# Sixteen rounds of value pages joined to eight pairs, in a decoder step on one core

## The chip, the core and the metric

The kernel runs on one core of one Trainium2 chip. The metric is the device time of one execution in microseconds (us); lower is better. Engines are named as the profile names them: PE is TensorE with its matrix products, PEld its loading of the stationary operand, DVE is VectorE, ACT is ScalarE, POOL is GpSimd, SP is SyncE, which here only issues transfers.

## What is computed

One layer of a decoder for 256 prompt tokens and 8 sequences of 4 new tokens (288 columns in all), model width 2048, in float32. The reference, cut to what matters:

```python
hp = ffn_half(hp, norm_ffn1[l], w_ffn1_gate[l], w_ffn1_up[l], w_ffn1_down[l])
cb, u, q, k, v, logf = mixer_in(hp, norm_mix[l], w_in[l], b_f[l])      # one projection, w_in
conv_y = cb * short_conv(u_ext, conv_w[l])
attn_o = fox_prompt(q, k, v, logf)
hp = mixer_out(hp, conv_y, attn_o, norm_conv_out[l], norm_attn_out[l], w_out[l])
hp = ffn_half(hp, norm_ffn2[l], ...)
hp = ple_add(hp, p_prompt[l], norm_ple[l], w_ple_gate[l], w_ple_proj[l])
# the new tokens go the same way, with this attention:
v_past = cache_v[page_table].reshape(DB, P, N_HEADS, HEAD_DIM)
s = jnp.einsum('bqhd,bkhd->bhqk', q, k_all, ...) * SCALE
s = s + Fq[..., None] - F[:, :, None, :]
p = jax.nn.softmax(s, axis=-1)
return jnp.einsum('bhqk,bkhd->bqhd', p, v_all)
```

The change touches the last line for the new tokens: probabilities times the values of the past. The past is 1024 rows a sequence, in 8 pages of 128 rows x 8 heads x 128 features, 0.524 MB each; 8 sequences have 64 pages, and a page table says where each lies.

## The kernel before

The 288 columns go through the whole layer together. A projection is made in output pairs of 2 x 128 rows, and a pair in **chunks**: four blocks of 128 input rows by 256 output columns, 0.524 MB of weights that SP loads into a place `raw0` to `raw7` (L238 to L247). ACT and DVE split every weight into a high and a low part (`whi`, `wlo`, L288), and PE makes three products for each block (L333 to L335), 24 for a chunk. The split runs up to five half chunks ahead of PE.

The order of the work in the mixing stage is written out by hand. A list `fill` holds the chunks: those of the keys, of the convolution's inputs, of the values and the first half of the output projection. A table `marks` says what stands ahead of chunk i: `at(i, f)` puts f at place i (L1003), and `between` (L978) merges both. `run_steps` (L352) goes through the steps, and ahead of each it asks for the loads of the next `state["ahead"]` items (`load_upto`, L232). An item is a weight, four key pages or, in this version, one value page. Each engine takes its instructions in the order that the scheduler of the framework makes of this; waits are put in by it.

The value pages go into eight places: `raw4` to `raw7`, three of their own (`v0` to `v2`) and `wideb` (`page_tile`, L260). From then on weights have only `raw0` to `raw3`, until the last round is done. The request for a page is an indirect transfer issued by POOL (L255), one instruction each, in POOL's order with its other work: the multiplications of the convolution (L901 to L945), the masks of the prompt's attention (L844, L845), the sums of squares (L889) and the additions into h (L1013).

The 64 pages are used in 16 **rounds** (`v_round`, L785): two groups of four sequences, eight rounds each, four pages a round, one of each sequence. A round is eight products of 32 columns by 512 on the four column groups of PE (`tile_position`), which the trace shows as 16 instructions at L794. They add up in two PSUM banks `va` through the eight rounds of a group; `sample_out` (L802) then adds the products with the new rows, and DVE picks out the heads. The rounds stand at places 51, 53, 56, 59, 61, 64, 67, 69, 72, 75, 78, 80, 83, 86, 88 and 91 (`VSTEP`, L1046), among `probs_t` (places 50 and 52), which transposes the probabilities, the natural forms of the values (L666), eight `prompt_head` (places 69, 71, 74, 76, 79, 81, 84, 86) and two norms. `v_start` (L966) at place 48 opens the stage and sets the lookahead to 12 items.

Of the kernel before, what the change touches and what calls it, by code (L numbers as in the profile page):

```python
# [36 lines left out]
PAGES = 8  # L37
# [10 lines left out]
KSTEP = 3  # L48
WEIGHTS = 4
VPAGES = 3  # L50
AHEAD = 12
WARM = (NT, NT, NT, P // 2)
VSTEP = 2.7

GAINS = ("norm_mix", "norm_ffn2", "norm_ple", "norm_final", "norm_conv_out", "norm_attn_out", "conv_w")
A_ROWS = dict(norm_mix=D, norm_ffn2=D, norm_ple=D, norm_final=D, norm_conv_out=CB * P, norm_attn_out=NH * P,
# [37 lines left out]
def build(nc, tc, ctx, A, O):  # L94
# [3 lines left out]
    v, s, g, pe, sy = nc.vector, nc.scalar, nc.gpsimd, nc.tensor, nc.sync  # L98
# [8 lines left out]
    def bank(tag, bufs):  # L107
        return ps.tile([P, 512], F32, name=tag, tag=tag, bufs=bufs)
# [28 lines left out]
    at = 0  # L137
# [15 lines left out]
    idx = cst.tile([P, 64], I32, name="idx")  # L153
# [76 lines left out]
    state = dict(wslot=0, pages=0, through=False, ahead=RAW, loaded=0, split=0, used=0, halves_used=0, chunk=0, lead=HALVES)  # L230

    def load_upto(n, parts=None):  # L232
        while state["loaded"] < min(n, len(items)):
            it = items[state["loaded"]]
            if it["kind"] == "p" and "vx" not in W:
                return
            if it["kind"] == "w":
                state["wslot"] = (state["wslot"] + 1) % (WEIGHTS if state["pages"] and not state["through"] else RAW)  # L238
                t = rawp.tile([P, it["nk"], 256], F32, name="wraw", tag=f"raw{state['wslot']}")
                src = it["src"]  # L240
                if parts is not None:
                    cuts = (0, 1, 2, 3, 4) if state["loaded"] < 2 else (0, 2, 4)
                    parts.append([(t[:, a:b], src[:, a:b]) for a, b in zip(cuts, cuts[1:])])
                else:
                    d = sy.dma_start(t, src)
                    if state["used"] < 24:
                        tc.keep_in_program_order(d)  # L247
            elif it["kind"] == "k":
                t = W["kt"][0].tile([P, 4, NH, P], F32, name="KT", tag="KT", bufs=2)
                for i, r in enumerate(it["rows"]):  # L250
                    g.indirect_dma_start(out=t[:, i].rearrange("p h s -> p (h s)"), out_offset=None, in_=it["src"],  # L251
                                         in_offset=bass.IndirectOffsetOnAxis(ap=r, axis=0))
            else:
                t = page_tile()
                g.indirect_dma_start(out=t, out_offset=None, in_=it["src"],  # L255
                                     in_offset=bass.IndirectOffsetOnAxis(ap=it["rows"], axis=0))
            it["tile"] = t
            state["loaded"] += 1

    def page_tile():  # L260

        own = ([(rawp, f"raw{i}") for i in range(WEIGHTS, RAW)] + [(W["vx"][0], f"v{i}") for i in range(VPAGES)]
               + [(W["mix"][0], "wideb")])
        n = state["pages"]
        state["pages"] += 1
        p, tag = own[n] if n < len(own) - 1 else own[(n + 1) % len(own)]
        return p.tile([P, 9 * P] if tag == "wideb" else [P, NH * P], F32, name="page", tag=tag)[:, :NH * P]

    halves = []
# [1 line left out]
    def split_upto(n):  # L271
        while state["split"] < min(n, len(halves)):
            it, j = halves[state["split"]]
            if "tile" not in it:
                return
            x = it["tile"][:, j:j + 2, :]
            hi = wsp.tile([P, 2, 256], F32R, name="whi", tag="whi")
            lo = wsp.tile([P, 2, 256], F32R, name="wlo", tag="wlo")
            if state["split"] < 4:
                it["parts"][j] = (hi, lo)  # L280
                state["split"] += 1
                continue
            split_weight(hi, lo, x, state["split"] < 14)
            it["parts"][j] = (hi, lo)
            state["split"] += 1
# [11 lines left out]
    def weight(src, k0, nk, c0):  # L297
        if len(src.shape) == 5:
            part = src[c0 // 256, k0 // 4]
        else:  # L300
            part = src[k0 * P:(k0 + nk) * P, c0:c0 + 256].rearrange("(k p) c -> p k c", p=P)
        return dict(kind="w", src=part, nk=nk, parts={})

    def page(src, j):
        return dict(kind="p", src=src, rows=idx[:, j:j + 1])

    def pair(src, c0, kts, act, evac, k_of=lambda k: k, late=0, tag="mm", rows_first=False):

        st = {}
        out = []  # L310
        chunks = [kts[i:i + 4] for i in range(0, len(kts), 4)]
        for ci, ks in enumerate(chunks):
            it = weight(src, ks[0], len(ks), c0)

            def fn(ci=ci, ks=ks, it=it, only=None):
                if ci == 0 and not only:
                    st["ps"] = [bank(tag, BANKS[tag]) for _ in range(2)]
                last = ci == len(chunks) - 1
                if only is None:
                    split_upto(state["halves_used"] + state["lead"])  # L320
                if not only:
                    state["chunk"] += 1
                for b in range(2):
                    o = st["ps"][b][:, :NT]
                    for j, k in enumerate(ks):
                        if only not in (None, j):
                            continue
                        hi, lo = it["parts"][j // 2 * 2]
                        w = slice(b * P, b * P + P)
                        xh, xl = act(k_of(k))  # L330
                        f = ci == 0 and j == 0
                        l = last and j == len(ks) - 1
                        pe.matmul(o, hi[:, j % 2, w], xh, start=f, stop=False)  # L333
                        pe.matmul(o, hi[:, j % 2, w], xl, start=False, stop=False)  # L334
                        pe.matmul(o, lo[:, j % 2, w], xh, start=False, stop=l)  # L335
                    if only not in (None, len(ks) - 1):
                        continue
                    if b == 0:
                        run_deferred()
                    if last and late:  # L340
                        defer(lambda b=b, o=o: evac(b, o), late)
                    elif last:
                        evac(b, o)
                state["halves_used"] += len(ks) // 2 if only is None else only % 2

            if rows_first:
                out.extend(([] if j else [it], lambda j=j, fn=fn: fn(only=j)) for j in range(len(ks)))
                continue
            out.append(([it], fn))
        return out  # L350

# [18 lines left out]
    def defer(fn, chunks=1):  # L370

        deferred.append((state["chunk"] + chunks, fn))

    def run_deferred(force=False):
        due = [d for d in deferred if force or d[0] <= state["chunk"]]
        for d in due:
            deferred.remove(d)
        for _, fn in due:
            fn()
# [55 lines left out]
    W = {}  # L435

    def opened(name, side="left"):
        st = ExitStack()
        W[name] = (pool(name, to=st, side=side), st)
# [91 lines left out]
    M = {}  # L531
# [250 lines left out]
                              t[:NS, :P].rearrange("s (c b x) -> s b c x", c=4, b=4)[:, b])  # L782
        M["PT", gi] = pt

    def v_round(gi, r):  # L785
        its = [page(A["cache_v"], (4 * gi + b) * PAGES + r) for b in range(4)]

        def fn():
            if r == 0:
                M["va", gi] = [bank("va", BANKS["va"]) for _ in range(2)]  # L790
                M["pv", gi] = M["PT", gi].rearrange("s (r b x) -> s r b x", b=4, x=32)
            for e in range(2):
                for b in range(4):
                    pe.matmul(M["va", gi][e][32 * b:32 * b + 32, :], M["pv", gi][:, r, b],  # L794
                              its[b]["tile"][:, e * 512:e * 512 + 512], start=r == 0, stop=False, tile_position=(0, 32 * b))
            if r == PAGES - 1:
                if gi == 1:
                    state.update(through=True, wslot=WEIGHTS - 1)
                sample_out(gi)
        return (its, fn)  # L800

    def sample_out(gi):  # L802
        mx = W["vv"][0]
# [162 lines left out]
    def v_start():  # L966
# [4 lines left out]
        opened("vx", "right")  # L971
        state["ahead"] = AHEAD
        vv = W["vv"][0]
# [29 lines left out]
    def at(i, *fns):  # L1003
        marks.setdefault(i, []).extend(fns)
# [37 lines left out]
    at(48, v_start)  # L1042
    at(50, lambda: probs_t(0))
    at(52, lambda: probs_t(1))
    for r in range(2 * PAGES):
        at(int(51 + VSTEP * r), v_round(r // PAGES, r % PAGES))  # L1046
    for hh in range(NH):
        at(int(69 + 2.5 * hh), lambda hh=hh: prompt_head(hh))
    at(80, lambda: norm_scale(rsc, acc2, CB * P, 2))
# [159 lines left out]
```

## Time and profile before

| | us |
|---|---|
| median of 3 runs | 2327.54 |
| lowest and highest | 2327.27, 2327.67 |
| the profiled execution | 2327.59 |
| its span, first to last instruction | 2325.8 |

The profile is one execution with the hardware profiler. Its rows read: start and length in us (timeline), engine, line of the kernel, operation, result and operands by the program's names, shape and count. A row of waits reads: who, waited for whom, us in total, times, longest. A row of a stretch reads: from and to, length, the busy time and number of instructions of PE, PEld, DVE, ACT and POOL, the granted clock of PE, the busy share of the 16 DMA engines, and GB/s. Queue q0 has POOL's transfers (among them the pages), q1 SP's (the weights). The stage with the value pages takes from about 1071 us, when the first page is asked for, to 1283 us.

### The profile page before, as it was taken

The numbers are of one execution on the slowest core, as the hardware profiler recorded it, in microseconds if no ns is written. First come the engines' busy times: TensorE is split into PE (matmuls) and PEld (weight loads), VectorE is DVE, ScalarE is ACT, GpSimd is POOL, SyncE is SP. The second block draws the span as 40 slices with busy tenths as digits, with TensorE's granted clock in tenths as the row PEclk, the third lists the DMA queues.
The fourth block names the chain that finished last, engine by engine and source line by source line (L and its number), as shares of the span: only waits on it lengthen the run. The fifth ranks groups of instructions, "written<-read, shape, count | busy, mean of one in ns | idle before, by whom it ended". The sixth has DMA issues, their size and how long they took to land.

```text
span 2325.8 us, 44305 instructions
## 1 busy us (share of the span) xinstructions
PE 2312.2 (99%) x17389; PEld 2254.0 (97%) x17389; DVE 1342.3 (58%) x2413; ACT 1057.1 (45%) x1864; POOL 323.9 (14%) x398
## 2 busy tenths in 40 slices
PE   9999999999999999999999999999999999999997
PEld 9999999999999999888888999999999999999997
DVE  7555555555555586456466765555555555555755
ACT  7444444444444453334344554444434444444654
POOL 1020000000000013444445210000000000000110
PEclk9999999999999999999999999999999999999999
DMA  8575555555555547997988555545555555555552
GB/s 273 164 238 166 166 167 164 164 165 166 167 164 164 163 163 232 330 318 262 321 316 295 164 165 158 176 155 172 163 166 164 170 164 164 164 165 167 164 166 91
DMA packets 342865, 443.44 MB, mean 191 GB/s; under 512 B 17424, under 2 KB 306976, under 8 KB 342656
## 3 DMA queue, kind: packets, MB, share of 16 engines
q1 hardware_dynamic: 320944, 366.32, 49.6%
q0 software_dynamic: 20480, 71.67, 9.0%
q8 instruction: 136, 2.23, 0.4%
q10 hardware_dynamic: 1232, 2.62, 0.3%
q14 instruction: 73, 0.60, 0.1%
HBM read 435.48 MB, written 5.07 MB: 189 GB/s over the span
## 4 chain that ended last, share of the span: by engine, by line
PE 99%; DVE 0%; ACT 0%; issue 0%; DVEq 0%
PE mm L333 31%; PE mm L335 31%; PE mm L334 31%; PE va L794 1%; PE va L736 1%; PE va L333 1%; PE va L335 1%; PE va L334 1%; DVE h L1135 0%; PE kt L335 0%; PE kt L333 0%; PE kt L334 0%; PE mm L509 0%; PE kt L848 0%; PE kt L881 0%; PE kt L872 0%
## 5 line engine op out<-in xcount | busy, mean ns | idle before, releaser
L288 DVE TENSOR_TENSOR wlo<-wraw,whi 128x512 fp32r<-128x512 f32 (+1 forms) x1388 | 973.0, 704 | 800.4 <-ACT whi L288 745.5
L288 ACT ACTIVATE whi<-wraw 128x512 fp32r<-128x512 f32 (+1 forms) x1388 | 866.3, 629 | 932.8 <-PE mm L334 864.0
L333 PE MATMUL mm<-xh,whi 128*128 128x288 f32 x3680 | 1094.3, 297 | 0.2 <-DVE uc L922 0.2
L334 PE MATMUL mm<-xl,whi 128*128 128x288 f32 x3680 | 1085.7, 295 | 0.0
L335 PE MATMUL mm<-xh,wlo 128*128 128x288 f32 x3680 | 1081.9, 294 | 0.0
L333 PEld LDWEIGHTS mm<-xh,whi 128*128 128x128 f32 x3680 | 689.7, 187 | 22.7 <-issue 17.3
L335 PEld LDWEIGHTS mm<-xh,wlo 128*128 128x128 f32 x3680 | 693.0, 188 | 0.1
L334 PEld LDWEIGHTS mm<-xl,whi 128*128 128x128 f32 x3680 | 691.0, 188 | 0.1
L333 PE MATMUL mm<-hh,whi 128*128 128x288 f32 x1408 | 416.8, 296 | 0.0
L334 PE MATMUL mm<-hl,whi 128*128 128x288 f32 x1408 | 415.4, 295 | 0.0
L335 PE MATMUL mm<-hh,wlo 128*128 128x288 f32 x1408 | 414.0, 294 | 0.0
L406 POOL TENSOR_TENSOR sr<-sg,rs 128x288 f32<-128x288 f32 x88 | 72.0, 820 | 1434.4 <-ACT sg L404 1434.2
L335 PEld LDWEIGHTS mm<-hh,wlo 128*128 128x128 f32 x1408 | 265.2, 188 | 0.0
L334 PEld LDWEIGHTS mm<-hl,whi 128*128 128x128 f32 x1408 | 264.4, 188 | 0.0
L333 PEld LDWEIGHTS mm<-hh,whi 128*128 128x128 f32 x1408 | 263.8, 187 | 0.0
L426 DVE SCALAR_TENSOR_TENSOR h<-mm,h 128x288 f32<-128x288 f32 x192 | 87.1, 455 | 23.4 <-PE mm L335 22.9
L251 POOL DMA_INDIRECT KT<-in_cache_k_dram,idx x64 | 66.4, 1038 | 127.3 <-DVE idx L162 53.2
L404 ACT ACTIVATE sg<-tg 128x288 f32<-128x288 f32 x88 | 39.0, 444 | 99.4 <-DVE tg L402 99.3
L413 ACT ACTIVATE hh<-hd 128x288 fp32r<-128x288 f32 x88 | 39.3, 446 | 93.7 <-DVE hd L411 93.6
L223 POOL TENSOR_TENSOR acc<-acc,sq 128x288 f32<-128x288 f32 x52 | 44.2, 850 | 226.9 <-ACT sq L222 224.5
L255 POOL DMA_INDIRECT page<-in_cache_v_dram,idx x64 | 64.4, 1006 | 71.6 <-PE va L794 50.2
L414 DVE TENSOR_TENSOR hl<-hd,hh 128x288 fp32r<-128x288 f32 x88 | 40.2, 458 | 22.0 <-ACT hh L413 22.0
(245 smaller groups left out, 1328.0 us busy)
## 6 DMA issues: line engine op xcount, KB each, us to landing
wraw<-in_w_ffn_gate_dram SPq DMA_DIRECT2D x172, 512.0 KB
wraw<-in_w_ffn_up_dram SPq DMA_DIRECT2D x172, 512.0 KB
wraw<-in_w_ffn_down_dram SPq DMA_DIRECT2D x160, 512.0 KB
wraw<-in_w_in_dram SPq DMA_DIRECT2D x96, 512.0 KB
wraw<-in_w_out_dram SPq DMA_DIRECT2D x32, 512.0 KB
wraw<-in_w_ple_gate_dram SPq DMA_DIRECT2D x32, 512.0 KB
wraw<-in_w_ffn_down_dram SPq DMA_DIRECT2D x32, 256.0 KB
wraw<-in_w_ple_proj_dram SPq DMA_DIRECT2D x8, 256.0 KB
```

Of the source, the lines that this page charges most:

```text
L223: (v if k >= KT - last_on_v else g).tensor_tensor(acc, acc, sq, ALU.add)
L251: g.indirect_dma_start(out=t[:, i].rearrange("p h s -> p (h s)"), out_offset=None, in_=it["src"], in_offset=bass.IndirectOffsetOnAxis(ap=r ...
L255: g.indirect_dma_start(out=t, out_offset=None, in_=it["src"], in_offset=bass.IndirectOffsetOnAxis(ap=it["rows"], axis=0))
L288: for i in s.activation(hi, x, AF.Copy), v.tensor_tensor(lo, x, hi.bitcast(F32), ALU.subtract):
L333: pe.matmul(o, hi[:, j % 2, w], xh, start=f, stop=False)
L334: pe.matmul(o, hi[:, j % 2, w], xl, start=False, stop=False)
L335: pe.matmul(o, lo[:, j % 2, w], xh, start=False, stop=l)
L404: s.activation(u, t, AF.Silu)
L406: g.tensor_tensor(r, u, rs, ALU.mult)
L413: s.activation(H["hi"][:, k, :], t, AF.Copy)
L414: v.tensor_tensor(H["lo"][:, k, :], t, H["hi"][:, k, :].bitcast(F32), ALU.subtract)
L426: v.scalar_tensor_tensor(h[:, k, :], o, 0.5, h[:, k, :], ALU.mult, ALU.add)
```

## The change

Two rounds are joined to a pair, `v_pair`, with no chunk between them. The eight pairs stand at places 54, 59, 64, 70, 75, 80, 86 and 91. Pages are no items any more: `v_load` asks for them at places of the table. The eight pages of a pair fill the eight places. Behind pair m's products two pages of the next pair are asked for; at the next place three more, with a wait for the last product of the chunk before it (`state["product"]`, added as a dependency), and at the place after that the last three with the same kind of wait. The first eight are asked for at places 48 (four), 50 (three) and 52 (one). The lookahead is 4 items from place 43 and, from place 48, 7 items, which are weights alone.

```diff
-AHEAD = 12
+AHEAD = 7
-VSTEP = 2.7
+VPAIRS = (54, 59, 64, 70, 75, 80, 86, 91)
...
-            if it["kind"] == "p" and "vx" not in W:
-                return
...
-            else:
-                t = page_tile()
-                g.indirect_dma_start(out=t, out_offset=None, in_=it["src"],
-                                     in_offset=bass.IndirectOffsetOnAxis(ap=it["rows"], axis=0))
...
-        p, tag = own[n] if n < len(own) - 1 else own[(n + 1) % len(own)]
+        p, tag = own[n % len(own)]
...
-                        pe.matmul(o, lo[:, j % 2, w], xh, start=False, stop=l)
+                        state["product"] = pe.matmul(o, lo[:, j % 2, w], xh, start=False, stop=l)
...
+    def v_load(a, b, after=None):
+
+        for n in range(a, b):
+            r, j = n // 4 % PAGES, (4 * (n // 32) + n % 4) * PAGES + n // 4 % PAGES
+            t = M["page", n] = page_tile()
+            d = g.indirect_dma_start(out=t, out_offset=None, in_=A["cache_v"],
+                                     in_offset=bass.IndirectOffsetOnAxis(ap=idx[:, j:j + 1], axis=0))
+            if after is not None:
+                tc.add_manual_dep(d.ins, after.ins.name, mybir.DependencyInfo(mybir.DependencyClass.Sync,
+                                                                              mybir.DependencyReason.DATA), reason="pace")
+
+    def v_pair(m):
+        for n in (2 * m, 2 * m + 1):
+            gi, r = n // PAGES, n % PAGES
...
                     pe.matmul(M["va", gi][e][32 * b:32 * b + 32, :], M["pv", gi][:, r, b],
-                              its[b]["tile"][:, e * 512:e * 512 + 512], start=r == 0, stop=False, tile_position=(0, 32 * b))
+                              M["page", 4 * n + b][:, e * 512:e * 512 + 512], start=r == 0, stop=False, tile_position=(0, 32 * b))
...
+        if m < 7:
+            v_load(8 * m + 8, 8 * m + 10)
...
-    for r in range(2 * PAGES):
-        at(int(51 + VSTEP * r), v_round(r // PAGES, r % PAGES))
+    at(43, lambda: state.update(ahead=WEIGHTS))
+    at(48, lambda: v_load(0, 4))
+    at(50, lambda: v_load(4, 7, state["product"]))
+    at(52, lambda: v_load(7, 8, state["product"]))
+    for m, i in enumerate(VPAIRS):
+        at(i, lambda m=m: v_pair(m))
+        if m < 7:
+            at(i + 1, lambda m=m: v_load(8 * m + 10, 8 * m + 13, state["product"]))
+            at(i + 2, lambda m=m: v_load(8 * m + 13, 8 * m + 16, state["product"]))
```

More of the change, by code (lines that the diff above doesn't have):

```diff
@@ L302, in weight @@
         return dict(kind="w", src=part, nk=nk, parts={})
-    def page(src, j):
-        return dict(kind="p", src=src, rows=idx[:, j:j + 1])
     def pair(src, c0, kts, act, evac, k_of=lambda k: k, late=0, tag="mm", rows_first=False):
@@ L783, in probs_t @@
         M["PT", gi] = pt
-    def v_round(gi, r):
-        its = [page(A["cache_v"], (4 * gi + b) * PAGES + r) for b in range(4)]
-        def fn():
+    def v_load(a, b, after=None):
[10 more added lines that the diff above has]
+            gi, r = n // PAGES, n % PAGES
             if r == 0:
@@ L799, in fn @@
                 sample_out(gi)
-        return (its, fn)
+        if m < 7:
+            v_load(8 * m + 8, 8 * m + 10)
     def sample_out(gi):
```

## The prediction, made before the result was known

> **What bounds the kernel now.** I read the page first: busy times and the chain of work that ended last.
>
> ```profile
> span 2325.8 us, 44305 instructions
> PE 2312.2 (99%) x17389; PEld 2254.0 (97%) x17389; DVE 1342.3 (58%) x2413; ACT 1057.1 (45%) x1864; POOL 323.9 (14%) x398
> PE 99%; DVE 0%; ACT 0%; issue 0%; DVEq 0%
> ```
>
> TensorE is the kernel: the chain of work that ended last is 99% PE. Then PE's own list of waits, which is short:
>
> ```profile
> PE mm L509 <- DVE eps L506: 1.2, 1, 1.2
> PE kt L1122 <- ACT sq L1108: 0.7, 1, 0.7
> PE mm L333 <- DVE uc L922: 0.2, 1, 0.2
> ```
>
> Three waits, 2.1 us in all, and only the 0.2 us could lie in the stage that is changed. So no page and no weight is late now, and the change can gain in one way alone: by making PE's stream of instructions shorter. It can lose by making PE wait. The timeline around the first round shows what a round costs (PE, then PE's weight loads):
>
> ```profile
> 1103.63 0.29 PE L334 MATMUL mm<-xl,whi 128*128 128x288 f32 x1
> 1103.76 0.29 PE L335 MATMUL mm<-xh,wlo 128*128 128x288 f32 x1
> 1103.99 1.92 PE L794 MATMUL va<-page,PT 128*32 128x512 f32 x16
> 1105.84 0.40 PE L333 MATMUL mm<-xh,whi 128*128 128x288 f32 x1
> 1106.08 0.29 PE L334 MATMUL mm<-xl,whi 128*128 128x288 f32 x1
> 1106.21 0.29 PE L335 MATMUL mm<-xh,wlo 128*128 128x288 f32 x1
> ...
> 1104.44 0.13 PEld L794 LDWEIGHTS va<-page,PT 128*32 128x32 f32 x4 [0.30 <-issue]
> 1104.87 0.13 PEld L794 LDWEIGHTS va<-page,PT 128*32 128x32 f32 x4 [0.30 <-issue]
> ```
>
> Columns are start and length in us. Ordinary products start 0.13 us apart. From the last product before the round (1103.76) to the second after it (1106.08) are 2.32 us; without the round they would be two steps, 0.27. A round costs **2.05 us**. Inside it, four column groups of 32 start together, and the next four follow 0.43 us later (1104.44, 1104.87): four such quarters, 1.72 us. The other 0.33 us is the way in (0.23 instead of 0.13 us) and the way out (the first product back is late and its successor follows after 0.24 us).
>
> **The change part by part.** *Joining.* A second round directly behind the first adds four quarters, 4 x 0.43 = 1.72 us, and no second way in and out. A pair costs 2.05 + 1.72 = 3.77 us, against 4.10 for two rounds. Eight pairs save 8 x 0.33 = **2.6 us**. The bound from the other side is nothing, if the seam between two rounds costs what a way in and out costs; every seam inside a round is a quarter step, so I take 2.6. The number of products, page loads and bytes is unchanged.
>
> *When the pages come.* Before, a page's request goes out as soon as the round that read its place is done, four at a time, while four other pages wait ready. Now all eight places are read in one pair and all eight are filled before the next. PE runs into whatever is late. The terms, from the rounds of before:
>
> ```profile
> 1113.41 0.64 PE L794 MATMUL va<-page,PT 128*32 128x512 f32 x4
> 1137.36 0.64 PE L794 MATMUL va<-page,PT 128*32 128x512 f32 x4
> 1158.11 0.64 PE L794 MATMUL va<-page,PT 128*32 128x512 f32 x4
> 1207.80 0.64 PE L794 MATMUL va<-page,PT 128*32 128x512 f32 x4
> 1231.13 0.64 PE L794 MATMUL va<-page,PT 128*32 128x512 f32 x4
> 1258.09 0.64 PE L794 MATMUL va<-page,PT 128*32 128x512 f32 x4
> 1280.80 0.64 PE L794 MATMUL va<-page,PT 128*32 128x512 f32 x4
> ```
>
> These are the rounds at places 53, 59, 64, 75, 80, 86 and 91 of the list of chunks. From 59 to 64 PE took 20.75 us, two rounds among it; with one pair instead it takes 20.75 - 0.33 = 20.4 us. From 53 to 59 it took 23.95 us with two rounds; the gap from 54 to 59 is one chunk (24 x 0.133 = 3.2 us) and 0.33 shorter, again 20.4. The other gaps are 75 to 80: 23.0; 80 to 86: 26.6; 86 to 91: 22.4; and 64 to 75 (49.7 us, four rounds) makes two gaps of over 24. **The first two gaps are the tight ones.**
>
> Call a pair's start S. How soon can data flow, and how fast? POOL's timeline around the round of 1137.36, the transfer view of the 2.9 us after 1138.2, and SP's timeline:
>
> ```profile
> 1139.54 0.94 POOL L255 DMA_INDIRECT page<-in_cache_v_dram,idx  x1 [7.23 <-PE va L794]
> 1140.78 0.94 POOL L255 DMA_INDIRECT page<-in_cache_v_dram,idx  x1 [0.30 <-issue]
> ...
> q1 hardware_dynamic: 190, 0.67, 68.6%
> page<-in_cache_v_dram,idx POOLq DMA_INDIRECT x2
> ...
> 1137.92 0.33 SPq L245 DMA_DIRECT2D wraw<-in_w_in_dram  x1
> 1143.17 0.33 SPq L245 DMA_DIRECT2D wraw<-in_w_in_dram  x1
> ```
>
> The request follows 2.2 us after the round began. Until 1141.1 the only queue with traffic is the weights' q1, though two pages are asked for: a page's bytes start 1.6 us after its request. So page data can flow from S + 3.8. It must be there when the second round of the next pair starts, S + 20.4 + 1.7. That leaves 18.3 us. Weights: one is asked for 0.6 us after the round began and the next only 5.3 us later, since PE uses none during a round. In a gap of five chunks one weight goes out at the start of the pair and is over by S + 3.8; four fall into the 18.3 us. Eight pages and four weights of 0.524 MB are 6.29 MB.
>
> What rate? Transfers of before, the stretches with the page queue full (last column GB/s, before it the busy share of the DMA engines), and what the two queues moved from 1141 to 1159:
>
> ```profile
> 1121.00:1138.00 17.00, 17.00 (x133) 14.86 (x136) 8.02 (x16) 6.32 (x10) 4.71 (x5) 1.00 0.95 354
> 1141.00:1159.00 18.00, 18.00 (x141) 15.61 (x143) 8.65 (x18) 6.21 (x10) 6.38 (x7) 1.00 0.95 336
> 1186.50:1191.00 4.50, 4.50 (x35) 4.45 (x35) 3.12 (x9) 2.71 (x6) 1.31 (x3) 1.00 1.00 401
> 1247.00:1260.00 13.00, 13.00 (x100) 11.30 (x98) 11.23 (x21) 6.95 (x15) 9.47 (x13) 1.00 0.84 286
> ...
> q0 software_dynamic: 1148, 4.18, 67.0%
> q1 hardware_dynamic: 481, 1.76, 26.7%
> ```
>
> The stretch 1141 to 1159 is the case itself: eight pages (4.18 MB) and 3.4 weights in 18 us. I take 345 GB/s, between the two long stretches: 6.29 MB need 18.2 us. The pacing takes time too: the third page is asked for when the chunk behind the pair ends, S + 3.8 + 3.2 = S + 7.0, so its data start at S + 8.6, while the first two (1.05 MB, alone) are in by about S + 3.8 + 3.2 = S + 7.0, at 330 GB/s. Up to 1.6 us the transfers idle, less where a weight fills them; I take 1.2. Later requests (S + 10.2 on) come while pages still wait, and cost nothing. So 18.2 + 1.2 = 19.4 us are needed and 18.3 are there: **1.1 us late**, in each of the first two gaps, 2.2 us together. At 354 GB/s it is 0.7 each, at 336 1.6, at 401 nothing. The gaps of 22.4 us and more have 2 us or more to spare, less 0.4 us for each prompt row (bk, 0.13 MB) in the same queue; I put them at nothing.
>
> [...]
>
> *What is moved in queues.* On POOL, a page request that waits stands ahead of the multiplications of the convolution, the prompt's masks and the adds into h. The new waits end with a product that PE issues before the result those need, so behind them only three requests (3 x 1.25 us by POOL's rows) delay them. DVE and ACT are under 60% busy, and POOL waits up to 7.2 us for a round now without PE waiting: nothing. If that cover were gone, DVE would stand up to 3.7 us for a mask. On SP nothing is added. The smaller lookahead from place 43 on only reorders what is emitted; the last weight that uses all eight places is that of chunk 50 as before. *First eight pages:* the first pair stands at place 54, not 51, and the last of its pages is asked for at place 52, two chunks (6.4 us) ahead; with the queue empty it needs 1.6 us and 0.524 MB at 345 GB/s, 1.5 us: nothing. *The end of the first group* moves from place 69 to 70 with its products of the new rows, its eight DVE instructions and the turn that is deferred by four chunks; their order to one another stays, and nobody waits for them before the second group: nothing.
>
> **Sum:** 2327.59 (the profiled execution: span 2325.8 and 1.8 us around it; the median of the runs is 2327.54) - 2.6 + 2.2 = **2327.1 us**. With the bounds of the rate: 2326.3 (354 GB/s) to 2328.2 (336).
>
> **The rivals.** *A: the whole gain.* With eight pages pending at once the transfers run at the 401 GB/s of the stretch from 1186.5, when four were pending: 6.29 MB in 15.7 us, 16.9 with the idle time, and no pair waits. 2327.59 - 2.6 = **2325.0**. For it speaks that stretch, against it that the stretches of 17 and 18 us had pages pending as well.
>
> *B: slower, by the cadence of the requests.* From 1247 to 1260 only 286 GB/s moved, because POOL put its adds between the requests:
>
> ```profile
> 1245.26 0.98 POOL L255 DMA_INDIRECT page<-in_cache_v_dram,idx  x1 [4.72 <-PE va L794]
> 1247.01 1.56 POOL L1013 TENSOR_TENSOR h<-h,tB 128x288 f32<-128x288 f32 x2
> 1248.72 1.23 POOL L255 DMA_INDIRECT page<-in_cache_v_dram,idx  x1
> ```
>
> If POOL's queue, with waits for products among its adds, spreads the eight requests that way in every gap, 6.29 MB take 22.0 us, 23.2 with the idle time: 4.9 us late in two gaps, about 2.3 in that of 23.0, 2.9 in that of 22.4, 1 each in those of 24: 17 us. 2327.59 - 2.6 + 17 = **2342**. It decides from 7.3 us of lateness on (4.65 net and the 2.6 of the joining), which is about 320 GB/s in all gaps with the idle time at its full 1.6 us. Against it: the two tight gaps lie before the adds into h begin, and the later gaps are longer.
>
> *C: it does not do what it says.* If other products are scheduled between the two rounds, the way in and out is paid sixteen times, and the lateness stays: 2327.59 + 0 to 2.2, **2328.7**. Against it: PE takes a helper's products in the order in which they are written, as all sixteen of a round above.
>
> **How the numbers follow.** The forecast 45%, A 28%, B 13%, C 9%; 5% for what I do not see, 3 of it on the faster side and 2 on the slower. The range reaches from A, less 0.4 for the run, to C with the 336 GB/s: 2324.6 to 2330.8; left out are B and the unseen, 18%. A measurement of this kernel tells some 0.2% (4.65 us) from no change. Faster by more than that needs more than the joining can give: 3%. Slower by more is B and the unseen: 15%. Within: 82%.
>
> **What would show it.** Right: sixteen-step rounds joined to thirty-two on PE's timeline, 3.77 us a pair; PE waiting for the page transfer ahead of the second and third pair by about 1 us each, in the second round, and at no other pair. Wrong: no such wait (A, and a rate of 370 or more in those gaps), waits at most pairs (B), or a wait of PE for DVE or ACT in this stage, which would mean that POOL's queue reaches further than I think. It is also wrong if a pair's length is not 3.77.

## The result, and the profile after

| | before | after |
|---|---|---|
| median of six runs, us | 2327.51 | 2336.96 |
| lowest and highest | 2327.27, 2328.54 | 2335.91, 2341.14 |
| the profiled execution | 2327.59 | 2336.4 |
| its span | 2325.8 | 2334.6 |

The ratio is 1.0043 with an interval of 1.0032 to 1.0054: the changed kernel is 0.43% slower, outside the predicted range of 2324.6 to 2330.8. The span grew by 8.8 us. Below are the rows of the page that answer to those shown of before (span, busy times, chain of work that ended last), then PE's own list of waits (who, for whom, us in total, times, longest).

```profile
span 2334.6 us, 44269 instructions
PE 2315.8 (99%) x17389; PEld 2255.1 (97%) x17389; DVE 1341.7 (57%) x2413; ACT 1057.5 (45%) x1864; POOL 325.5 (14%) x398
PE 97%; issue 1%; POOL 1%; DVE 0%; DMA 0%; ACT 0%; DVEq 0%; POOLq 0%
```

```profile
PE va L795 <- DMA page<-in_cache_v_dram,idx: 5.3, 3, 4.8
PE mm L500 <- DVE eps L497: 1.2, 1, 1.2
PE kt L1131 <- ACT sq L1117: 0.7, 1, 0.7
```

The chain is no longer PE alone, and a new wait stands at the head of the list: PE waits for value pages three times, 5.3 us in all, 4.8 of them at once. The busy time grew by 3.6 us as well with the same 17389 products, so some of them became slower or no longer ran side by side. The two sit side by side on PE's timeline at the first pair (start, length, number of instructions, idle time before them and what ended it):

```profile
1114.32 1.92 PE L795 MATMUL va<-page,PT 128*32 128x512 f32 x12
1116.17 0.40 PE L324 MATMUL mm<-xh,whi 128*128 128x288 f32 x1
...
1116.67 0.29 PE L324 MATMUL mm<-xh,whi 128*128 128x288 f32 x1
1121.72 5.03 PE L795 MATMUL va<-page,PT 128*32 128x512 f32 x20 [4.75 <-DMA page<-in_cache_v_dram,idx]
1126.68 0.40 PE L325 MATMUL mm<-xl,whi 128*128 128x288 f32 x1
```

The pair is torn in two: twelve products, then four products of a chunk, 4.75 us of nothing, then the other twenty. From its start to the first product behind it are 1126.68 - 1114.32 = 12.36 us, less 0.53 for the four chunk products 11.83. An undisturbed pair, the fifth, with the chunk's products around it:

```profile
1214.83 0.29 PE L326 MATMUL mm<-xh,wlo 128*128 128x288 f32 x1
1215.06 3.64 PE L795 MATMUL va<-page,PT 128*32 128x512 f32 x32
1218.63 0.40 PE L324 MATMUL mm<-xh,whi 128*128 128x288 f32 x1
1218.87 0.30 PE L325 MATMUL mm<-xl,whi 128*128 128x288 f32 x1
```

It takes 1218.63 - 1215.06 = 3.57 us. So the first pair costs 8.26 us too much. Twenty products should take five quarters (steps of up to four products side by side), 5 x 0.43 = 2.15 us and the end of the last one; they took 5.03. The granted clock says why (the stretch view; the column behind POOL's is the clock):

```profile
1121.70:1125.00 3.30, 3.28 (x17) 0.88 (x18) 0.00 (x0) 0.00 (x0) 0.00 (x0) 0.56 0.68 263
1125.00:1128.00 3.00, 3.00 (x18) 1.54 (x13) 0.00 (x0) 0.00 (x0) 0.00 (x0) 1.00 0.00 0
```

For about 3 us after the wait PE ran at half its clock: four quarters took 0.855, 0.853, 0.853 and 0.587 us from start to start instead of 0.43. And the quarters were broken, since the missing page held back one of the four column groups: four steps of three products ahead of the wait and four of a single product behind it, each as long as a full quarter (0.43 to 0.54 us). By the starts of the single products, the wait is 4.9 us of the 8.26, the half clock 1.43, the four extra steps 1.7, and a second way in and out 0.2.

The second pair and the last one, with a row of the weight loads (PEld) of the last:

```profile
1142.98 2.78 PE L795 MATMUL va<-page,PT 128*32 128x512 f32 x22
1146.14 1.90 PE L795 MATMUL va<-page,PT 128*32 128x512 f32 x10 [0.38 <-DMA page<-in_cache_v_dram,idx]
1147.98 0.40 PE L324 MATMUL mm<-xh,whi 128*128 128x288 f32 x1
...
1287.13 4.42 PE L795 MATMUL va<-page,PT 128*32 128x512 f32 x32
1291.48 0.66 PE L809 MATMUL va<-vs,PT 32*32 32x512 f32 x8
...
1289.64 0.21 PEld L795 LDWEIGHTS va<-page,PT 128*32 128x32 f32 x8 [0.65 <-DMA page<-in_cache_v_dram,idx]
```

The second takes 5.00 us (1142.98 to 1147.98), the third 4.78, the last 4.35. PE's own list has no wait for the last one, but its quarters are broken into threes and ones, and the weight load of its last page waited 0.65 us for the transfer. So this is a late page too, hidden behind the two quarters (0.86 us) that the other three column groups still had to do: in the second pair they began these at 1144.73 and 1145.16 and then stood still until the page's products at 1146.14. In total: joining -2.64, first pair +8.26, second +1.42, third +1.21, last +0.78, and -0.2 elsewhere, which is +8.8.

### The profile page after: what moved, and what is told of

Read it like the earlier page. It is cut to its first block, busy times and chain, and to the rows that moved or that the text cites. A ratio compares the mean times of both kernels' runs of the same rounds, so it can differ in the third digit from the quotient of the medians.

```text
span 2334.6 us, 44269 instructions
## 1 busy us (share of the span) xinstructions
PE 2315.8 (99%) x17389; PEld 2255.1 (97%) x17389; DVE 1341.7 (57%) x2413; ACT 1057.5 (45%) x1864; POOL 325.5 (14%) x398
## 4 chain that ended last, share of the span: by engine, by line
PE 97%; issue 1%; POOL 1%; DVE 0%; DMA 0%; ACT 0%; DVEq 0%; POOLq 0%
PE mm L324 31%; PE mm L326 30%; PE mm L325 30%; PE va L727 1%; PE va L795 1%; PE va L324 1%; PE va L326 1%; PE va L325 1%; POOL page L781 1%; DMA page<-in_cache_v_dram,idx 0%; DVE h L1144 0%; PE kt L324 0%; PE kt L326 0%; PE kt L325 0%; PE kt L883 0%
## 5 line engine op out<-in xcount | busy, mean ns | idle before, releaser
L417 DVE SCALAR_TENSOR_TENSOR h<-mm,h 128x288 f32<-128x288 f32 x192 | 87.2, 455 | 23.3 <-PE mm L326 22.9
```

What stands on the lines that cost most here:

```text
L417: v.scalar_tensor_tensor(h[:, k, :], o, 0.5, h[:, k, :], ALU.mult, ALU.add)
```

## Why the fourth page was late

POOL's timeline shows the requests of the first pair's pages, and SP's the weights asked for in the same time (for each, start, length, count, wait):

```profile
1099.92 1.14 POOL L781 DMA_INDIRECT page<-in_cache_v_dram,idx  x1 [1.85 <-PE mm L326]
...
1105.15 1.33 POOL L781 DMA_INDIRECT page<-in_cache_v_dram,idx  x1 [0.31 <-DVE wlo L282]
1108.94 0.94 POOL L781 DMA_INDIRECT page<-in_cache_v_dram,idx  x1 [2.46 <-DVE wlo L282]
...
1111.93 1.01 POOL L781 DMA_INDIRECT page<-in_cache_v_dram,idx  x1 [0.16 <-ACT sq L946]
...
1116.20 1.16 POOL L781 DMA_INDIRECT page<-in_cache_v_dram,idx  x1 [1.42 <-DVE wlo L282]
```

```profile
1070.49 11.92 SPq L243 DMA_DIRECT2D wraw<-in_w_in_dram  x4
```

The last request went out at 1116.20, 1.9 us after its pair had begun, and it had waited for DVE's part of a weight's split. Before that, four weights had been asked for from 1070.49 on. By the order of the code they are those of chunks 51 to 54. `v_start` at place 48 raises the lookahead from 4 to 7, and `run_steps` asks for the loads of the next items ahead of every step, so the weights of 52 to 54 are asked for along with that of 51 before `v_load(0, 4)`, while `state["pages"]` is still 0 and weights still rotate through all eight places. Before, chunk 50's weight was the last of those, in `raw3`; counted on from there, those of 51 to 54 take `raw4` to `raw7`, the places of pages 0 to 3. Page 3 then waits for the split of chunk 54's weight, and that chunk stands *behind* the first pair. That was my **theory by place**. The rivals: the rate or the cadence of the requests, the gap between pairs, and the pacing.

## The experiments

The kernel before, run on the same chips, had medians of 2327.40, 2327.49 and 2327.43 us over 22, 33 and 21 runs.

### 1. Pages first

```diff
 def v_start():
-    state["ahead"] = AHEAD
...
 at(48, lambda: v_load(0, 4))
+at(48, lambda: state.update(ahead=AHEAD))
```

> The lookahead is raised from 4 to 7 items only behind the first four page requests, so that the weights of chunks 52 to 54 no longer go into raw5 to raw7 ahead of the pages. Place theory (the fourth page of the first pair waits for raw7, where the weight of chunk 54 lies, a chunk that PE reaches only behind that pair): no wait of 4.75 us, no half clock, no split first pair; the 8.3 us of the first pair go, the lateness of 1.4 and 1.2 us at the second and third pair and 0.8 at the last stays: 2337.0 - 8.3 = 2328.7 us, spread of the runs under 1 us. Rival (POOL's order and the pacing make the page late): the first pair still waits, 2335 us or more.

Measured: 2327.77 us (2326.61 to 2331.82), ratio 1.0004 (0.9995 to 1.0014); 9.2 us of the 9.4 are gone. The spread of under 1 us that was expected did not come: it is 5.2 us. SP's timeline over the same time as above has two weights instead of four ahead of 1085, and PE's timeline has the first pair whole:

```profile
1070.01 15.12 SPq L243 DMA_DIRECT2D wraw<-in_w_in_dram  x2
```

```profile
1113.84 4.45 PE L795 MATMUL va<-page,PT 128*32 128x512 f32 x32
1118.22 0.40 PE L324 MATMUL mm<-xh,whi 128*128 128x288 f32 x1
```

No wait for a page is left on PE's list. The pair takes 4.38 us, not 3.57: quarters of three and one. The second, third and last are broken likewise, 0.79, 0.58 and 0.35 us too long. On the list of the weight loads these four pairs still wait for pages, up to 0.7 us each: the pages are late, but by less than the other columns cover.

### 2. Wider gaps

```diff
 (experiment 1, and)
-VPAIRS = (54, 59, 64, 70, 75, 80, 86, 91)
+VPAIRS = (54, 60, 66, 71, 76, 81, 86, 91)
```

> As the one before, and the pairs at 54, 60, 66, 71, 76, 81, 86, 91: no gap under 21.5 us by the rounds of before, where the two tight ones had 20.4. If pages are late in a gap by its length alone, the 2.6 us of the second and third pair go, those of the last (gap of 21.8) stay and the fourth (21.5) may gain up to 1: 2328.7 - 2.6 + 0.5 = 2326.6 us, between 2325.5 and 2327.5. If the lateness has another cause (a bound of the transfers over the whole stage), it moves to other pairs: 2328.5 or more.

Measured: 2336.33 us (2333.11 to 2337.47), ratio 1.0033 (1.0021 to 1.0045). A miss, and an instructive one: the lateness moved to other pairs, as the rival said. Pairs 1 to 3, now 23.6 and 24.3 us apart, are undisturbed at 3.57. But the fourth, 21.1 us behind the third, took 10.28 us, the seventh 6.74 and the eighth 6.50, though their gaps were 23.3 and 25.5 us. The transfers of the fourth pair's gap (queue: packets, MB, share; then who asked, KB):

```profile
DMA packets 2238, 8.09 MB, mean 346 GB/s; under 512 B 251, under 2 KB 251, under 8 KB 2236
...
q0 software_dynamic: 1217, 4.41, 53.6%
q1 hardware_dynamic: 699, 2.54, 28.3%
q10 hardware_dynamic: 320, 1.11, 11.7%
...
wraw<-in_w_in_dram SPq DMA_DIRECT2D x5, 512.0 KB
out_dram<-vn ACTq DMA_DIRECT2D x1, 1024.0 KB
page<-in_cache_v_dram,idx POOLq DMA_INDIRECT x9
```

In the 23.4 us from the first page's data to the last byte 8.09 MB moved at 346 GB/s, near my 345. That the two agree is partly luck: it is the mean of 279 GB/s up to 1175, 362 up to 1182 and 418 behind. But beside the eight pages and some five weights there lay 1.1 MB of new value rows written out, which my 6.29 MB for a gap do not have. So the bytes are a matter of the place. (That the writing did it is read from this view; it was not moved by itself.) The seventh pair, which began at 1260.55, is another case. POOL's requests around it, and the transfers from 1241 to 1265:

```profile
1248.52 0.94 POOL L781 DMA_INDIRECT page<-in_cache_v_dram,idx  x1 [0.30 <-issue]
...
1254.95 1.37 POOL L781 DMA_INDIRECT page<-in_cache_v_dram,idx  x1
...
DMA packets 1845, 6.69 MB, mean 279 GB/s; under 512 B 216, under 2 KB 216, under 8 KB 1844
```

The last three pages were asked for 6.4 us after the fifth, as POOL did its adds into h and its masks in between, and only 279 GB/s moved. That is the cadence of the prediction's rival B, in a gap of 23.3 us.

### 3. A lookahead of 6

```diff
-AHEAD = 7
+AHEAD = 6
```

> The changed kernel with a lookahead of 6 in place of 7, nothing else: the weights of chunks 51 to 53 lie in raw4 to raw6, that of 54 in raw0. Place theory: the last page request of the first pair comes one split earlier, some 3 to 4 us, so the wait falls from 4.75 us to 0.5 to 1.5, too short for the half clock: 2337.0 - 4 - 1.4 = 2331.6 us, between 2330 and 2333. Rival (order and pacing): the same as the changed kernel within 1 us, 2336 to 2338.

Measured: 2330.34 us (2328.70 to 2334.03), ratio 1.0013 (1.0004 to 1.0022). One item less of lookahead, everything else as changed, takes away 6.6 of the 9.4 us. By pairs: the first, 8.26 us too long, is now 0.92 too long, with no wait on PE's list, as the last weight in eight places is now one that PE uses ahead of the pair. The second, third, sixth and last are 2.02, 1.63, 1.39 and 0.53 too long, so what is left lies there.

### 4. Joining alone

```diff
 (the kernel before)
-        at(int(51 + VSTEP * r), v_round(r // PAGES, r % PAGES))
+        at(VPAIRS[r // 2], v_round(r // PAGES, r % PAGES))
```

> The kernel before with its sixteen rounds at the places of the pairs, two at each, and its own requests (lookahead of 12 items, a page asked for as soon as its place is free, no pacing). Joining saves 2.6 us; pages of the first pair come behind the weight of chunk 53 in the list, which then lies in raw6: by the place theory a wait of 0 to 1.5 us at the first pair. The tight gaps cost 1.5 to 2.6 us. 2327.5 - 2.6 + 3 = 2328 us, between 2326.5 and 2331. If the cost of the change came from the pacing and the lookahead alone, with no late page here: 2324.9.

Measured: 2340.88 us (2339.65 to 2342.46), ratio 1.0057 (1.0043 to 1.0071). A second miss. PE's waits, and the sum of the stretches from 1100 to 1300:

```profile
PE kt L881 <- ACT pT L874: 2.3, 2, 1.2
PE mm L333 <- issue: 1.9, 3, 1.0
PE va L794 <- DMA page<-in_cache_v_dram,idx: 1.7, 1, 1.7
PE mm L333 <- ACT whi L288: 1.4, 1, 1.4
...
sum 200.00, PE 189.75 PEld 159.29 DVE 113.11 ACT 73.68 POOL 91.58; mean PE 18.98 PEld 15.93 DVE 11.31 ACT 7.37 POOL 9.16
```

By the last bytes of their queue, the pages land 4 to 14 us ahead of their use, but for the first pair; yet PE idles 10.25 us. Its list puts 4.6 us of them down to ACT and DVE, which stand still themselves for up to 10.1 us, 1.7 to a page and 3.6 to nothing that it can name. The old way of asking does not carry pairs, so the new one does some work. Why ACT stood still is not settled; bursts of requests alone don't do it, by experiment 5.

### 5. No pacing

```diff
 (experiment 1, and)
-            if after is not None:
+            if False:
```

> The kernel with the pages asked for ahead of the raised lookahead, and the pacing of the requests by the products taken away: a pair's next eight pages are asked for as soon as their places come free. Two theories. If what made joining alone slow (2340.9 us) was that the requests came in bursts that nothing paced, this kernel loses likewise: 2332 us or more, with no wait of PE for a page and more idle time of PE before the other stages' products. If pacing only delays pages, the broken quarters of the first, second, third and last pair (2.7 us in all over the undisturbed 3.57 us of a pair) shrink: 2325.5 to 2327.8 us.

Measured: 2325.69 us (2324.94 to 2326.44), ratio 0.9993 (0.9984 to 1.0002). Seven pairs take 3.57 us and the second 3.80; PE waits for no page, and once, 0.6 us, for a split. The same gaps of 20.4 us are wide enough without pacing, but for 0.23 us. In them 355 GB/s moved (1117.8 to 1136.4 and 1138.2 to 1156.1); the stretches of 1120 to 1140 and 1140 to 1160, which reach beyond them, show 349 and 329.

### 6. The order of a pair's products kept

```diff
 (experiment 1, and)
-                    pe.matmul(M["va", gi][e][...], ...)
+                    tc.keep_in_program_order(pe.matmul(M["va", gi][e][...], ...))
```

> The kernel with the pages asked for ahead of the raised lookahead, and the 32 products of a pair kept in the order in which the program writes them, so that a page that the planner expects late can't break the quarters of four. Theory: the first, second, third and last pair each cost 0.35 to 0.8 us more than the others because their quarters are broken up, not because a page is late; then every pair takes 3.57 us and the time is 2325.1 us (2324.6 to 2325.8). Rival: the order was broken because a page really is late, and a wait takes the place of the extra quarters: 2327 to 2329 us, with waits for pages at these pairs.

Measured: 2330.38 us (2327.99 to 2333.36), ratio 1.0013 (1.0004 to 1.0022). The rival holds: the pages really are late. PE's timeline at the second pair, and the load for its last page, here and in experiment 1 (the last row):

```profile
1135.30 2.78 PE L796 MATMUL va<-page,PT 128*32 128x512 f32 x22
1139.06 1.90 PE L796 MATMUL va<-page,PT 128*32 128x512 f32 x10 [0.99 <-DMA page<-in_cache_v_dram,idx]
1140.90 0.40 PE L324 MATMUL mm<-xh,whi 128*128 128x288 f32 x1
...
1139.06 0.16 PEld L796 LDWEIGHTS va<-page,PT 128*32 128x32 f32 x8 [1.90 <-DMA page<-in_cache_v_dram,idx]
...
1137.60 0.20 PEld L795 LDWEIGHTS va<-page,PT 128*32 128x32 f32 x8 [0.66 <-DMA page<-in_cache_v_dram,idx]
```

With the fixed order the second and third pair wait 1.2 and 1.4 us (by the starts of their products) and are 2.03 and 2.27 too long, against 0.79 and 0.58 in the free order. But at the second pair the order of the loads is the same in both: four quarters of four, two steps of three, then the late page. So the edit changed no order there, and the difference is that the page came 1.2 us later in this execution, counted from the start of the pair. Broken quarters are no way around a late page; they are what one looked like while its load waited less than the 0.86 us of two quarters (0.66 in experiment 1), and a wait came on top when it waited longer (1.90 here, of which PE shows 0.99). Why the pages came later here is open. The first pair is whole, at 3.57 us.

### 7 and 8. Earlier pairs, and the same with the order kept

```diff
 (experiment 1, and)
-    at(43, lambda: state.update(ahead=WEIGHTS))
+    at(43, lambda: state.update(ahead=3))
...
-    at(52, lambda: probs_t(1))
-    at(50, lambda: v_load(4, 7, state["product"]))
-    at(52, lambda: v_load(7, 8, state["product"]))
+    at(51, lambda: probs_t(1))
+    at(49, lambda: v_load(4, 7, state["product"]))
+    at(51, lambda: v_load(7, 8, state["product"]))
...
-VPAIRS = (54, 59, 64, 70, 75, 80, 86, 91)
+VPAIRS = (52, 58, 64, 70, 75, 80, 85, 91)
```

> Pages asked for ahead of the raised lookahead, and the first pairs moved forward (places 52, 58, 64, 70, 75, 80, 85, 91, the first requests moved forward too), so that every gap between pairs is at least 23 us by the places of the kernel before. Theory by the gap: with 23 us and more no pair is late or broken, and all the gain of joining is left: 2325 us (2324.5 to 2326). Rival by place: what comes late depends on what else is queued at that place (bias rows, other pages, POOL's own work), as in the run with wider gaps, whose fourth, seventh and eighth pair waited: 2328 to 2336 us, with waits for pages at some later pair.

> The same with the pair's products kept in the order of the program. Theory by the gap: nothing is late, and the order is whole: 2324.9 us (2324.4 to 2325.6). Rival by place: waits for pages at later pairs as in the kernel without the fixed order: 2328 us or more.

Measured: 2325.36 us (2324.96 to 2327.35) and 2325.70 (2324.59 to 2326.47), both with the ratio 0.9993 (0.9984 to 1.0002). The page of experiment 7 and its second pair:

```profile
span 2323.2 us, 44269 instructions
...
PE 2309.8 (99%) x17389; PEld 2254.4 (97%) x17389; DVE 1343.1 (58%) x2413; ACT 1058.5 (46%) x1864; POOL 325.8 (14%) x398
```

```profile
1131.76 3.64 PE L795 MATMUL va<-page,PT 128*32 128x512 f32 x32
1135.33 0.40 PE L324 MATMUL mm<-xh,whi 128*128 128x288 f32 x1
```

From the second on all pairs take 3.57 us; the first takes 4.37 (3.84 with the order kept). The span is 2.6 us under that before, as much as joining was to save, although the first pair still lost 0.80; by the sum below it would be 0.7 us longer.

### 9 and 10. No pacing, with the earlier pairs and with the change as it was

```diff
 (9: experiment 7; 10: the changed kernel; and in both)
-            if after is not None:
+            if False:
```

> The best of the runs so far put together: pages asked for ahead of the raised lookahead, first pairs earlier so that all gaps are 23 us or more, and no pacing of the requests. Theory that each late page costs only itself: the one pair still broken with the earlier places (the first, 4.37 us against 3.57) becomes whole, or nothing changes: 2324.5 to 2325.5 us. Rival, that the pacing keeps pages out of the way of the weights: a wait of PE for a weight's split, as the unpaced run shows one of 0.6 us, and 2325.7 us or more.

> The changed kernel with the pacing alone taken away, the lookahead raised ahead of the first requests as it was. Theory by place: the fourth page of the first pair has the place of chunk 54's weight and still waits for that weight's split, so the first pair keeps its 8 us, and only the second, third and last pair gain (up to 3.4 us): 2333 to 2335.5 us, with one wait of PE for a page of 4 to 5 us. Rival, that the pacing by the products makes the first page late: the wait is gone and the time is 2325.5 to 2328 us.

Measured: 9: 2325.95 us (2325.12 to 2326.41), ratio 0.9993 (0.9984 to 1.0002), above the expected 2324.5 to 2325.5. The first pair is whole, the second is 0.26 us late, and PE waits 0.3 us for a split, as the rival said. 10: 2331.63 us (2329.23 to 2334.31), ratio 1.0018 (1.0009 to 1.0027). PE's timeline at its first pair, and a stretch of it:

```profile
1114.50 1.92 PE L795 MATMUL va<-page,PT 128*32 128x512 f32 x12
...
1120.03 5.12 PE L795 MATMUL va<-page,PT 128*32 128x512 f32 x20 [2.88 <-DMA page<-in_cache_v_dram,idx]
1125.08 0.40 PE L325 MATMUL mm<-xl,whi 128*128 128x288 f32 x1
...
1120.00:1123.00 3.00, 2.97 (x16) 0.78 (x17) 0.00 (x0) 0.00 (x0) 0.10 (x1) 0.50 0.96 381
```

The wait of the first pair stays, though shorter than expected (2.9 us, not 4 to 5, and the time below the expected 2333), half clock and torn quarters with it: 6.5 us too long. The other seven pairs are all at 3.57. So the late page of the first pair belongs to the place, and the late pages of the second, third and last pair to the pacing.

One sum holds through nearly all of these: the span of before, less 2.64 for the joining, plus what each pair takes over 3.57 us. It gives 2334.8 for the changed kernel (span 2334.6), 2325.7 for experiment 1 (2325.3), 2329.6 for 3 (2329.2), 2336.5 for 2 (2335.7), 2327.8 for 6 (2328.2), 2323.4 for 5 (2323.6), 2323.9 for 7 (2323.2) and 2329.6 for 10 (2330.2). Only joining alone falls out of it, as most of its loss lies outside the pairs.

## Why the prediction was wrong, point by point

- **Joining, 0.33 us a pair: right.** By the prediction's own measure, from the last product before the pair (1214.83) to the second behind it (1218.87), a pair adds 4.04 - 0.27 = 3.77 us, as forecast.
- **"the last weight that uses all eight places is that of chunk 50 as before": the step that failed.** It is that of chunk 54 (with the lookahead of 4 alone it would be 51, as in experiment 1). I took the smaller lookahead from place 43 for the whole story and did not follow the order at place 48, where the lookahead is raised before the first page is asked for. Hence "First eight pages ... nothing" cost 8.26 us, nearly all of the miss. Undoing that order alone (experiment 1) took away 9.2 of 9.4 us; one item less of lookahead (3) took 6.6. Even then "nothing" is too little: in experiment 1 the first pair still lost 0.81 us to a late page.
- **The tight gaps, 1.1 us late each: right in size.** The changed kernel lost 1.42 and 1.21 us there, in the second round of the pairs, as forecast. The size varies: 0.79 and 0.58 in experiment 1, 2.03 and 2.27 in 6. Its two terms hold too: without pacing, 18.2 of 18.3 us are needed, and experiments 5 and 10 lose at most 0.23 us in these gaps; with 23 us (2 and 7) nothing is lost.
- **"I put them at nothing", of the other gaps: right here except for the last pair**, whose late page cost 0.78 us; the sixth lost 1.39 in experiment 3, and experiment 2 shows that the bytes of a gap and the cadence of its requests depend on its place.
- **The price of a late page was too low at the first pair.** I counted only the lateness. That held for a short one: the second pair's page came 1.2 us later in experiment 6 than in 1, and the pair took 1.24 us more. At the first pair the long wait also brought the half clock (1.43 us), and the torn pair took four more steps (1.7 us) and a second way in and out (0.2).
- **Rivals:** A's number, 2325.0, nearly came once the order was mended and the pacing taken away or the first pairs moved (2325.4 to 2326.0), but not by A's mechanism: the tight gaps of experiment 5 ran at 355 GB/s, not at 401. B's cadence was not the cause here: lateness at most pairs did not come, and in experiment 1 no pair lost more than 0.81 us. With other places (2) it did show at the seventh pair. C didn't occur: thirty-two steps stand together in seven of eight pairs.

Experiments 5, 7, 8 and 9 beat both kernels by their medians: 1.5 to 2.1 us under before, with most single runs below the lowest of before. But each interval reaches from 0.9984 to 1.0002, so a gain is likely and not proven.

## What to carry to other kernels

Where two kinds of tile share places in turn, write down for each place its last reader under the new order of requests, from the first request on; a lookahead raised one line too early can hand a place to work that stands behind its next user. An operand that was several us late cost more than the wait here: to 4.9 us of waiting came 1.43 us for the half clock and 1.7 for the steps that weren't full. One that was a little late stood on no list of PE's waits, only on that of its weight loads (0.65 us in the last pair): look at both. And bytes between two points are counted at that place, with what is written out, not taken from another gap.

## What the runs showed of the hardware

The half clock came after a wait of 4.75 us (granted clock 0.56 over the next 3.3 us) and also after 2.88 us (0.50 over 3 us), and in experiment 2 after two waits of 0.97 and 1.97 us with one product group between them (0.50 from 1190 to 1193 us); it did not after 1.67 us in experiment 4 (1.00 from 1122 to 1124) or after up to 1.0 us, by PE's list, in 3 (1.00 from 1139 to 1141 and from 1161 to 1163). In the changed kernel the granted clock was 1.00 from 1120 to 1121, in the wait, 0.50 from 1121.2 to 1124.5 and 1.00 again from 1124.6 on, 2.9 us after the first product behind the wait. How long a single wait must be for it was not measured between 1.67 and 2.88 us.

Four products of 32 columns on the four column groups took 0.43 us together (1288.01 to 1288.44 in the last pair of the changed kernel); three took 0.43 us too (1288.87 to 1289.30), and so did one alone (1290.53 to 1290.96). A step that wasn't full saved nothing. But the column groups kept their own pace: in that pair the late group's products began at 1289.64, 1290.10, 1290.53 and 1290.96, and the other three ran beside them, from 1289.73 and 1290.16.

Kernels with late pages scattered more: 2335.9 to 2341.1 for the changed one and 2329.2 to 2334.3 for experiment 10, against less than 1.8 us between the lowest and highest of before on a chip.
